# Low weight parts of the second layer kept in DRAM, and its second half's layer norm held until the gates are through

## The chip, the cores and the metric

The kernel runs on one core of one Trainium2 chip. The metric is device time in microseconds for one launch. TensorE (PE in the rows) multiplies; VectorE (DVE) and ScalarE (ACT) do the elementwise work; GpSimd (POOL) does a few small pieces; SyncE (SP) issues every DMA of this kernel, in one queue.

## The reference

Two layers over 2048 positions of 1024 features, all in float32. Layer 0 has attention and pooling branches; layer 1 is the convolution module that the change is about.

```
def odd_mixer(h, w_in, dw_w, dw_b, ln_g, ln_b, w_out):
    proj = h @ w_in
    a, b, gate = jnp.split(proj, [CONV_WIDTH, 2 * CONV_WIDTH], axis=-1)
    glu = a * jax.nn.sigmoid(b)
    conv = lax.conv_general_dilated(
        glu, dw_w.astype(glu.dtype), window_strides=(1,), padding=[(CONV_K - 1, 0)],
        dimension_numbers=('NWC', 'WIO', 'NWC'), feature_group_count=CONV_WIDTH)
    cf = conv.astype(jnp.float32) + dw_b.astype(jnp.float32)
    mu = jnp.mean(cf, axis=-1, keepdims=True)
    var = jnp.mean(jnp.square(cf - mu), axis=-1, keepdims=True)
    cn = (cf - mu) * lax.rsqrt(var + EPS) * ln_g.astype(jnp.float32) + ln_b.astype(jnp.float32)
    y = jax.nn.silu(cn).astype(h.dtype) * jax.nn.silu(gate)
    return y @ w_out
...
    for layer in range(DEPTH):
        h = rms_norm(x, pre_norm[layer])
...
        x = x + rms_norm(y, post_norm[layer])
```

## The kernel before

**Products in three matmuls.** Every float32 operand of a projection is held as a high part (rounded to `fp32r`) and a low part (the rest, also `fp32r`). A product is high times high, high times low and low times high: three matmuls of 128x512 for each of 8 slices of the contraction, 24 for one 128-feature output tile of 512 positions. For a weight of 128x1024 (512 KB), SP loads the raw tile `wr` (3 buffers), ACT copies it into the high part `wh` (2 buffers), and DVE subtracts to make the low part `wl` (2 buffers). `w_split` does that in the fixed order `wseq`; `project` takes the pair and issues the 24 matmuls.

**Stages.** The sequence is cut into two halves of 1024 positions, each into two blocks of 512 (b0, b1). Layer 0 does half 0 and half 1 in turn. In layer 1 each half goes through the input projections (`inproj1`, weights `wc` 0 to 15, each used for two blocks, so 48 matmuls a weight) and the gates (`gates1`, `wc` 16 to 23). Then comes the output projection (`outproj`, weights `wo1` 0 to 7): half 0 b0, half 0 b1, half 1 b0, each loading all 8 weights again, 24 matmuls a weight; and half 1 b1 as two pieces of 256 columns (`last_block`) that share one set of weights. So layer 1 loads and splits 48 + 32 = 80 weight tiles, though only 32 are different.

**The convolution and the norm.** Five of the eight feature tiles are convolved on DVE (`conv_dve`, 31 taps of 128x1024 each), three on TensorE (`conv_pe`). Results go to DRAM (`cd_*`, `ct_*`), the gates' values too (`sg_*`). `norms` loads the eight tiles of a half back (`s4` buffers), adds them for the mean, subtracts the mean and sums squares (`norm_block`), and then, tile by tile, `apply` multiplies by the reciprocal deviation, applies SiLU, multiplies by the gate and splits the product into high and low part (`mix`), which `outproj` multiplies. `post_norm` (tiles `xr`, `x1_*`, `out_y`) follows each output block.

**What sets the order.** A planner (`Flow`) writes the program while Python runs: generator tasks with priorities are stepped when the planner's own clocks say that their data are there; nothing is ordered by hand. A waiting task is stepped only when DVE and ACT are at most `LAG` ahead of TensorE in the plan. On the chip every engine then takes its list strictly in order. Buffers (`s4`: 37 of 4.2 KB a partition) are counted by `avail`, and a DMA into a buffer stands in SP's queue with a wait for the buffer's last reader. A weight's two buffers are free for weight n+2 when TensorE has done the last matmul of weight n.

Of the kernel before, what the change touches and what calls it, by code (L numbers as in the profile page):

```python
# [5 lines left out]
F32 = mybir.dt.float32  # L6
U8 = mybir.dt.uint8
F32R = mybir.dt.float32r
AF = mybir.ActivationFunctionType
ALU = mybir.AluOpType  # L10
# [31 lines left out]
    "mm": 4, "a0": 1, "a1": 1, "pt": 1, "pv": 1,  # L42
}
PACK = (
    ("sinks", 8), ("post", 2 * KT), ("icnt", 64), ("tri", 2 * P), ("pscale", 4), ("dwn", len(DVE_CONV) * CK), ("dwb", KT), ("dwbp", KT * GPT),
    ("lng", KT), ("lnb", KT),
)
LAG = 1.0
# [159 lines left out]
def trunk_kernel(tc, a):  # L208
# [38 lines left out]
    def get(tag, cols=TH, dt=F32):  # L247
        while avail[tag] <= 0:
            yield None
        if tag in ("a0", "a1", "pt", "pv") and freed[tag]:  # L250
            at = freed[tag][0]
            while avail[tag] <= 0 or at + MARGIN > flow.t["P"]:
                yield at if avail[tag] > 0 else None
                if freed[tag]:
                    at = freed[tag][0]
        return make(tag, cols, dt)
# [16 lines left out]
    def until(cond):  # L273
        while not cond():
            yield None
# [44 lines left out]
    for h in range(NH):  # L320
        wseq += [("wo1", f) for b in range(NB) for f in range(KT)]
    wraw, wready, last = [], [], set()

    def w_load(go):
        for n, (name, i) in enumerate(wseq):
# [29 lines left out]
    def w_split():  # L355
        for n in range(len(wseq), 0, -1):
            yield from until(lambda: wraw)
            name, i, raw, at = wraw.pop(0)
            yield from until(lambda: at)
            yield at[0]  # L360
            if name == "wut":
                raw = yield from fold(i, raw)
            if n > KT - 2 and n != len(wseq) - 2:
                wh = yield from get("wh", dt=F32R)
                wl = yield from get("wl", dt=F32R)
            else:
                yield from until(lambda: n > KT or len(last) == KT * NB)
                wh = (yield from get("s4", TH, F32R)).rearrange("p (k f) -> p k f", k=KT)
                wl = (yield from get("s4", TH, F32R)).rearrange("p (k f) -> p k f", k=KT)
            for j, ks in enumerate(WPARTS if n == len(wseq) else WHOLE):  # L370
                yield from until(lambda: len(at) > j)
                yield at[j]
                yield A.activation(wh[:, ks], raw[:, ks], AF.Copy)
                V.tensor_tensor(out=wl[:, ks], in0=raw[:, ks], in1=wh[:, ks].bitcast(F32), op=ALU.subtract)
                if j == 0:
                    wready.append((name, i, wh, wl))
            put(raw)
# [100 lines left out]
    def halves(t):  # L478
        return t[:, :BL], t[:, BL:]
# [100 lines left out]
    rb0 = {}  # L580
    flow.spawn(w_load(go), 0)
    flow.spawn(w_split(), 0)
    for b in range(NB):
        flow.spawn(prep_first(b, hs, have, go), 1 + b)
    flow.wait(lambda: len(go) == NB)
# [462 lines left out]
    def conv_pe(i, over):  # L1048
        gs, tts, nt = [], [], [0]
        for e in range(2):  # L1050
            g = (yield from get("s4", GPT // 2 * (GS + 2))).rearrange("x (r s) -> x r s", r=GPT // 2)
            G.memset(g[:, :, :2], 0.0)
            at = Q.dma_start(out=g[:, :, 2:], in_=gt[i][e * GPT // 2:(e + 1) * GPT // 2].rearrange("r x s -> x r s"))
            gs.append((g, at))
        for o in range(GPT // 4):
            bk = yield from get(f"a{o % 2}")
            for u in range(2):
                while len(tts) < 2 and nt[0] < GPT // 2:
                    tt = yield from get("s4", 2 * NJ * P)
                    r = 2 * nt[0]  # L1060
                    tts.append((tt, Q.dma_start(out=tt.rearrange("x (r n) -> x r n", r=2), in_=a["toep"][PE_CONV.index(i), r:r + 2].rearrange("r x n -> x r n"))))
                    nt[0] += 1
                tt, at = tts.pop(0)
                yield max(at, gs[o // 2][1])
                for v in range(2):
                    r4 = 2 * u + v
                    g = gs[o // 2][0][:, (o % 2) * 4 + r4]
                    for j in range(NJ):
                        at = T.matmul(bk[:, r4 * P:(r4 + 1) * P], tt[:, (v * NJ + j) * P:(v * NJ + j + 1) * P], g[:, 2 - j:2 - j + GS], start=j == 0, stop=j == NJ - 1)
                put(tt)  # L1070
            if o % 2:
                put(gs[o // 2][0])
            yield at
            co = yield from get("t2")
            for r4 in range(4):
                r = 4 * o + r4
                at = A.activation(co[:, r4 * P:(r4 + 1) * P], bk[:, r4 * P:(r4 + 1) * P], AF.Identity, bias=dwbp[:, i * GPT + r:i * GPT + r + 1], scale=1.0)
            put(bk)
            yield at
            Q.dma_start(out=cp_t[i][4 * o:4 * o + 4].rearrange("r x s -> x r s"), in_=co.rearrange("x (r s) -> x r s", r=4))  # L1080
            put(co)
        for h in range(NH):
            over[h].append(i)
# [51 lines left out]
    def apply(half, k, b, cfs, rbs, sgs, mix, done, left):  # L1135
        c = cfs[k][:, cols(b)]
        yield V.tensor_tensor(out=c, in0=c, in1=rbs[b], op=ALU.mult)
        yield A.activation(c, c, AF.Silu, bias=lnb[:, k:k + 1], scale=lng[:, k:k + 1])
        key = (k // 2, b)
        if key not in sgs:  # L1140
            yield from until(lambda: (half, *key) in stored)
            g = yield from get("s4")
            sgs[key] = (g, Q.dma_start(out=g, in_=sg_t[(half, *key)]))
        g, at = sgs[key]
        yield at
        yield V.tensor_tensor(out=c, in0=c, in1=halves(g)[k % 2], op=ALU.mult)
        t = yield from get("s4", TH, F32R)
        mix[b][k] = t
        hi, lo = halves(t)
        yield A.activation(hi, c, AF.Copy)  # L1150
        V.tensor_tensor(out=lo, in0=c, in1=hi.bitcast(F32), op=ALU.subtract)
        done.add((k, b))
        for tile, key in ((g, (k // 2, b)), (cfs[k], k)):
            left[key] = left.get(key, 0) + 1
            if left[key] == 2:
                put(tile)

    def norms(half, over, mix, done):
        yield from until(lambda: len(over[half]) >= 5 and (half == 0 or len(dones[half - 1]) >= KT))
        cfs, rbs, sgs, left, loaded = {}, {}, {}, {}, []  # L1160

        def load():
            for n in range(KT):
                yield from until(lambda: len(over[half]) > n)
                k = over[half][n]
                c = yield from get("s4")
                if k in DVE_CONV:
                    at = Q.dma_start(out=c, in_=cd_t[k, half])
                else:
                    view = cp_t[k].rearrange("r x s -> (r x s)").rearrange("(c q s) -> c q s", c=P, q=PH)  # L1170
                    at = Q.dma_start(out=c.rearrange("c (q s) -> c q s", q=PH), in_=view[:, :, half * SG:(half + 1) * SG])
                cfs[k] = c
                loaded.append((c, at))

        flow.spawn(load(), 1)
        total = yield from get("s4")
        for n in range(1, KT):
            yield from until(lambda: len(loaded) > n)
            c, at = loaded[n]
            yield at  # L1180
            V.tensor_tensor(out=total, in0=loaded[0][0] if n == 1 else total, in1=c, op=ALU.add)
        cfs["sum"] = total
        yield flow.t["V"]

        def block(b):
            yield from norm_block(b, cfs, rbs)
            yield from spread_tasks([apply(half, k, b, cfs, rbs, sgs, mix, done, left) for k in range(KT)], 3, 1 + b)
            put(rbs[b])

        for b in range(NB):  # L1190
            flow.spawn(block(b), 1 + b)
        yield from until(lambda: len(rbs) == NB)
        put(total)

    stored = set()

    def gate_out(half, j, b, sg, ready):
        yield from until(lambda: ready[0] == 2)
# [50 lines left out]
    for half in range(NH):  # L1249
        inproj1(half, hs, have, over)  # L1250
        now = hs
        hs, have = [{} for _ in range(NB)], [set() for _ in range(NB)]
        if half + 1 < NH:
            flow.spawn(prep(1, half + 1, hs, have, 2), 2)
        else:
            for h in range(NH):
                flow.spawn(norms(h, over, mixes[h], dones[h]), 1)
        gates1(half, now)
    for half in range(NH):
        outproj(1, half, mixes[half], dones[half])  # L1260
    flow.wait(lambda: not flow.tasks)
# [84 lines left out]
```

## Time and profile before

| what | us |
|---|---|
| median of 3 runs (1500.33 to 1501.77) | 1501.53 |
| the profiled execution, whole time | 1503.71 |
| its span, first to last instruction | 1500.8 |
| TensorE busy in the span (98%) | 1469.3 |
| VectorE busy (83%) | 1250.2 |
| ScalarE busy (38%) | 565.2 |

The profiled execution is one run; its whole time is its span and 2.9 us around it. "Busy" of TensorE counts an instruction from its start to its modelled end, so overlapping matmuls give a full share; pace is read better from the starts of successive matmuls. Idle time shows only as a gap between instructions.

### The profile page before, as it was taken

How to read it: one execution, taken by the hardware profiler on the slowest of the kernel's cores; microseconds unless marked ns; L12 is line 12 of the kernel's file. 1: busy time of each engine (PE TensorE's matmuls, PEld its weight loads, DVE VectorE, ACT ScalarE, POOL GpSimd, SP SyncE). 2: the span in 40 equal slices, each digit the busy share in tenths (PEclk: the TensorE clock that was granted, in tenths of full speed). 3: DMA queues.
4: the chain of work that ended last, by engine and by line, in shares of the span. 5: the costliest groups of instructions: out<-in, count | busy, mean ns of one | idle time of the engine just before them, and what ended most of it. 6: DMA issues, size and time to landing. Idle time of an engine off the chain costs nothing.

```text
span 1500.8 us, 19112 instructions
## 1 busy us (share of the span) xinstructions
PE 1469.3 (98%) x7226; PEld 1193.0 (79%) x7226; DVE 1250.2 (83%) x1927; ACT 565.2 (38%) x1069; POOL 49.1 (3%) x65
## 2 busy tenths in 40 slices
PE   8999999999999999999999999999999999998997
PEld 6877778788877778788888888888888888776796
DVE  7888775777887766577899999999999999989885
ACT  6454432454444423454211123211212134666551
POOL 0000000000000000000100000000000000000000
PEclk9999999999999999999999999999999999999898
DMA  6112312455411101355421224422544744836574
GB/s 221 57 54 80 97 44 59 140 175 176 145 33 33 46 29 56 99 178 187 166 63 55 82 85 136 172 71 67 182 148 137 236 144 137 256 127 229 165 251 154
DMA packets 107468, 186.46 MB, mean 124 GB/s; under 512 B 32240, under 2 KB 56432, under 8 KB 107376
## 3 DMA queue, kind: packets, MB, share of 16 engines
q1 hardware_dynamic: 107376, 185.25, 39.3%
q8 instruction: 56, 0.92, 0.3%
q14 instruction: 36, 0.29, 0.1%
HBM read 146.42 MB, written 38.80 MB: 123 GB/s over the span
## 4 chain that ended last, share of the span: by engine, by line
PE 92%; DVE 3%; DMA 2%; ACT 1%; issue 1%; SPq 0%; POOL 0%; POOLq 0%; DVEq 0%; ACTq 0%
PE mm L189 81%; PE a L189 5%; PE pv L189 3%; PE pt L189 2%; DVE s L189 2%; DMA s<-in_toep 1%; DVE t L189 1%; DVE wl L189 0%; DMA s<-in_xn 0%; DMA gt<-s 0%; ACT s L189 0%; DMA s<-sg 0%; SPq L189 0%; ACT wh L189 0%; ACT t L189 0%
## 5 line engine op out<-in xcount | busy, mean ns | idle before, releaser
L189 PE MATMUL mm<-s,wh 128*128 128x512 f32 (+1 forms) x3616 | 1139.6, 396 | 13.3 <-ACT s L189 7.4
L189 PEld LDWEIGHTS mm<-s,wh 128*128 128x128 f32 x3616 | 669.5, 189 | 164.6 <-DVE s L189 10.7
L189 PE MATMUL mm<-s,wl 128*128 128x512 f32 (+1 forms) x1808 | 709.9, 393 | 0.0
L189 PEld LDWEIGHTS mm<-s,wl 128*128 128x128 f32 x1808 | 341.4, 189 | 76.2
L189 DVE SCALAR_TENSOR_TENSOR s<-s,packed,s 128x1024 f32<-128x1024 f32 x290 | 354.6, 1279 | 0.0
L189 ACT ACTIVATE wh<-wr 128x1024 fp32r<-128x1024 f32 (+1 forms) x138 | 145.4, 1054 | 368.8 <-PE mm L189 315.9
L189 DVE TENSOR_TENSOR wl<-wr,wh 128x1024 fp32r<-128x1024 f32 (+1 forms) x138 | 167.7, 1215 | 74.9 <-ACT wh L189 72.8
L189 ACT ACTIVATE t<-mm 128x512 f32<-128x512 f32 (+1 forms) x122 | 68.5, 562 | 98.6 <-PE mm L189 90.3
L189 DVE TENSOR_TENSOR t<-t,t 128x512 f32<-128x512 f32 (+1 forms) x131 | 86.2, 663 | 17.3 <-ACT t L189 15.4
L189 ACT ACTIVATE s<-mm 128x512 f32<-128x512 f32 (+1 forms) x116 | 67.9, 585 | 78.2 <-PE mm L189 70.8
L189 PE MATMUL a<-s,s 128*128 128x128 f32 (+2 forms) x592 | 90.5, 290 | 1.1 <-DMA s<-in_toep 0.9
L189 PEld LDWEIGHTS a<-s,s 128*128 128x128 f32 x592 | 81.1, 190 | 11.1 <-DMA s<-in_toep 2.8
L189 DVE TENSOR_TENSOR s<-s,s 128x512 f32<-128x512 f32 (+3 forms) x100 | 85.0, 874 | 3.3 <-DMA s<-ct 1.0
L189 ACT ACTIVATE s<-t 128x512 fp32r<-128x512 f32 (+1 forms) x52 | 48.8, 938 | 64.4 <-DVE t L189 64.1
L189 DVE TENSOR_TENSOR s<-t,s 128x512 fp32r<-128x512 f32 (+1 forms) x56 | 52.4, 935 | 22.1 <-ACT s L189 20.9
L189 ACT ACTIVATE t<-s 128x512 f32<-128x512 f32 x80 | 48.8, 628 | 50.7 <-DVE s L189 42.4
L189 DVE TENSOR_TENSOR t<-pt,packed 128x512 f32<-128x512 f32 x64 | 44.1, 690 | 28.4 <-PE pt L189 27.9
L189 ACT ACTIVATE s<-s,st 128x128 f32<-128x128 f32 x128 | 49.6, 389 | 25.0 <-DVE st L189 24.9
L189 POOL TENSOR_TENSOR rs<-ms,mhalf 128x4 f32<-128x4 f32 (+1 forms) x21 | 24.9, 1186 | 791.8 <-DVE ms L189 787.7
L189 DVE SCALAR_TENSOR_TENSOR s<-t,mm 128x512 f32<-128x512 f32 x48 | 40.1, 836 | 8.1 <-PE mm L189 6.2
L189 ACT ACTIVATE s<-xh 128x512 fp32r<-128x512 f32 x48 | 29.9, 630 | 39.9 <-DVE xh L189 39.5
L189 PEld LDWEIGHTS pv<-t,s 128*64 128x64 f32 x480 | 25.1, 136 | 23.2 <-issue 7.2
(100 smaller groups left out, 928.3 us busy)
## 6 DMA issues: line engine op xcount, KB each, us to landing
wr<-in_wo SPq DMA_DIRECT2D x64, 512.0 KB, 3.7
wr<-in_wc SPq DMA_DIRECT2D x48, 512.0 KB, 3.7
wr<-in_wa SPq DMA_DIRECT2D x27, 512.0 KB, 3.7
s<-in_toep SPq DMA_DIRECT2D x24, 384.0 KB, 4.3
xr<-in_xp SPq DMA_DIRECT2D x32, 256.0 KB, 4.1
x<-s SPq DMA_DIRECT2D x32, 256.0 KB, 3.2
xh<-x SPq DMA_DIRECT2D x32, 256.0 KB, 3.6
sg<-s SPq DMA_DIRECT2D x16, 512.0 KB, 4.8
```

The source lines that it names most:

```text
L189: fn(*args, **kw)
```

## The change

Before, the low part of each layer-1 weight is made anew on DVE each time that the weight is used. Now a task `w_lows` of the lowest priority makes the 32 different ones once (load, ACT copy, DVE subtract) and stores them to DRAM; 29 are stored while layer 0 runs and three in the first projections of layer 1. In layer 1 `w_split` issues a 512 KB DMA into the `wl` buffer where DVE subtracted. Also, `norms` of half 1 starts when `gates1` of half 1 is written (`gated`) and no longer when half of half 0's products are there; each norm loads at most about three tiles ahead of its sum; half 1's norm tasks are one priority lower; `apply` leaves three `s4` buffers free before that point; and the bias table `dwbp` holds only the three convolutions on TensorE.

```diff
+    lows = [x for n, x in enumerate(wseq) if x[0] in ("wc", "wo1") and x not in wseq[:n]]
+    kept = {(name, i): dr.tile([P, KT, P], F32, tag=f"{name}l_{i}", name=f"{name}l_{i}") for name, i in lows}
+    formed = set()
+
+    def w_lows():
+        yield 60.0
+        for name, i in lows:
+            yield from until(lambda: avail["s4"] > 5)
+            raw = (yield from get("s4")).rearrange("p (k f) -> p k f", k=KT)
+            wl = (yield from get("s4", TH, F32R)).rearrange("p (k f) -> p k f", k=KT)
+            yield Q.dma_start(out=raw, in_=a[name][i])
+            yield A.activation(wl, raw, AF.Copy)
+            at = V.tensor_tensor(out=wl, in0=raw, in1=wl.bitcast(F32), op=ALU.subtract)
+            put(raw)
+            yield at
+            Q.dma_start(out=kept[name, i], in_=wl.bitcast(F32))
+            put(wl)
+            formed.add((name, i))
...
                 yield at[j]
+                if (name, i) in kept:
+                    yield from until(lambda: (name, i) in formed)
+                    Q.dma_start(out=wl.bitcast(F32), in_=kept[name, i])
                 yield A.activation(wh[:, ks], raw[:, ks], AF.Copy)
-                V.tensor_tensor(out=wl[:, ks], in0=raw[:, ks], in1=wh[:, ks].bitcast(F32), op=ALU.subtract)
+                if (name, i) not in kept:
+                    V.tensor_tensor(out=wl[:, ks], in0=raw[:, ks], in1=wh[:, ks].bitcast(F32), op=ALU.subtract)
...
+    flow.spawn(w_lows(), 6)
...
-            yield from until(lambda: (half, *key) in stored)
+            yield from until(lambda: (half, *key) in stored and (avail["s4"] > 3 or gated))
...
+        yield from until(lambda: avail["s4"] > 3 or gated)
         t = yield from get("s4", TH, F32R)
...
-        yield from until(lambda: len(over[half]) >= 5 and (half == 0 or len(dones[half - 1]) >= KT))
+        yield from until(lambda: len(over[half]) >= 5 and (half == 0 or gated))
...
-                yield from until(lambda: len(over[half]) > n)
+                yield from until(lambda: len(over[half]) > n and added[0] >= n - 2)
...
+            added[0] = n
...
-            flow.spawn(block(b), 1 + b)
+            flow.spawn(block(b), 1 + b + half)
...
         gates1(half, now)
+    gated.append(1)
```

Three places of the program show what moved. Names carry the buffer's number; `s4_` are the general buffers.

**DVE, at half 1 b0 of the output projection, before.** `wl_1732` is the low part of weight 1 for that block; `s4_1734` is the fourth of the block's eight products, `s4_1742`, `s4_1744` the next two; `ms_1743` belongs to the statistics of half 0 b1's output, which TensorE has finished when this block begins; between them stand pieces of `post_norm` (`xr_`).

```order
L189 TENSOR_TENSOR wl_1732_10910<-wr_1708_10770,wh_1731_10909 128x1024
L189 TENSOR_TENSOR s4_1734_10923<-s4_1589_10151,s4_1734_10923 128x512
L189 TENSOR_TENSOR s4_1624_10343<-s4_1624_10343,xr_1728_10887 128x512
...
L189 TENSOR_TENSOR t2_1662_10547<-t2_1662_10547,t2_1738_10947 128x512
L189 TENSOR_SCALAR ms_1743_10963<-pt_1740_10951 128x4
L189 TENSOR_TENSOR t2_1662_10547<-t2_1662_10547,t2_1741_10956 128x512
L189 TENSOR_TENSOR s4_1742_10961<-s4_1588_10149,s4_1742_10961 128x512
L189 TENSOR_TENSOR s4_1744_10970<-s4_1590_10153,s4_1744_10970 128x512
```

**DVE, the same place, now.** `s4_1813` and `s4_1814` are the seventh and eighth product of half 1 b0, `s4_1815` the first of b1; `ms_1825` is the same statistics of half 0 b1.

```order
L189 TENSOR_TENSOR s4_1813_11184<-s4_1681_10506,s4_1813_11184 128x512
L189 TENSOR_TENSOR s4_1684_10537<-s4_1684_10537,s4_1795_11094 128x512
L189 TENSOR_TENSOR s4_1651_10358<-s4_1651_10358,s4_1796_11101 128x512
L189 TENSOR_TENSOR s4_1653_10362<-s4_1653_10362,s4_1796_11101 128x512
L189 TENSOR_TENSOR s4_1814_11196<-s4_1684_10537,s4_1814_11196 128x512
L189 TENSOR_TENSOR s4_1815_11202<-s4_1651_10358,s4_1815_11202 128x512
...
L189 TENSOR_SCALAR ms_1825_11268<-pt_1824_11256 128x4
```

Five of the eight products stood behind the low part of weight 1; now all eight stand ahead of the statistics, and no low part is among them.

**SP, at the start of the output projection, now.** `wl_1646` is the low part of weight 1 and `wl_1659` that of weight 2 for half 0 b0; `cd_`, `ct_` are convolved tiles of half 1, `sg_0_` gates of half 0 that are loaded, `sg_1_3_1` one that is stored.

```order
L189 DMA wl_1646_10341<-wo1l_1_133 128x1024
L189 DMA wr_1649_10351<-in_wo1 128x1024
L189 DMA s4_1651_10358<-cd_0_1_79 128x1024
L189 DMA s4_1652_10360<-ct_2_75 128x16x64
L189 DMA s4_1653_10362<-cd_1_1_81 128x1024
L189 DMA s4_1655_10367<-sg_0_0_1_89 128x1024
L189 DMA s4_1656_10369<-sg_0_1_1_91 128x1024
L189 DMA sg_1_3_1_103<-s4_1632_10230 128x1024
L189 DMA wl_1659_10397<-wo1l_2_134 128x1024
```

Behind these stand `wr_1662`, `cd_3`, `ct_4`, then `wl_1667` (weight 3), `wr_1668`, an `sg_` load, `cd_5`, `wl_1677` (weight 4), `wr_1678`, `ct_6`, an `sg_` load, `cd_7` and `wl_1687` (weight 5). Before, the same loads of half 1 stand in one run there, with weights' raw tiles around them and no low part.

**SP, at the last block, now.** `s4_1886` and `s4_1887` are the residual input for its first piece, `wl_1890` the low part of weight 1.

```order
L189 DMA wl_1880_11570<-wo1l_0_132 128x1024
L189 DMA wr_1883_11580<-in_wo1 128x1024
L189 DMA s4_1886_11603<-x1_1_1_107 128x4x256
L189 DMA s4_1887_11604<-x1_1_1_107 128x4x256
L189 DMA wl_1890_11612<-wo1l_1_133 128x1024
L189 DMA wr_1892_11627<-in_wo1 128x1024
```

The residual loads stand ahead of a low part that did not go through this queue before.

## Rows read from the trace of the kernel before

**Rows 1.** The page's first lines: span, and busy us (share) of each engine.

```profile
span 1500.8 us, 19112 instructions
PE 1469.3 (98%) x7226; PEld 1193.0 (79%) x7226; DVE 1250.2 (83%) x1927; ACT 565.2 (38%) x1069; POOL 49.1 (3%) x65
```

**Rows 2.** Windows: stretch, length; busy (count) by engine; granted clock, DMA share, GB/s.

```profile
0.00:750.00 750.00, 739.25 (x3740) 588.26 (x3741) 560.52 (x1160) 329.24 (x684) 23.97 (x38) 1.00 0.33 104
750.00:1250.00 500.00, 498.97 (x2311) 410.75 (x2310) 478.39 (x449) 106.56 (x177) 15.63 (x20) 1.00 0.40 121
```

**Rows 3.** Windows of the output projection of layer 1, same columns.

```profile
1282.40:1328.90 46.50, 45.69 (x195) 36.31 (x194) 41.88 (x51) 26.77 (x41) 0.00 (x0) 1.00 0.78 239
...
1379.50:1403.90 24.40, 16.96 (x48) 12.06 (x48) 19.78 (x36) 9.94 (x15) 2.83 (x2) 0.65 0.49 169
1403.90:1439.90 36.00, 36.00 (x158) 29.29 (x157) 32.17 (x47) 22.49 (x35) 0.00 (x0) 1.00 0.72 231
```

**Rows 4.** Timeline of PE there: start, length, what, [idle before it, who ended it].

```profile
1380.86 0.50 PE L189 MATMUL mm<-s,wh 128*128 128x512 f32 x1 [0.89 <-DVE s L189]
...
1385.28 1.68 PE L189 MATMUL pt<-ones,t 128*128 128x1 f32 x8 [3.69 <-DVE t L189]
...
1389.41 0.80 PE L189 MATMUL mm<-s,wh 128*128 128x512 f32 x1 [1.14 <-DVE s L189]
```

**Rows 5.** Chain that ended last, one piece: start, length, matmuls run without a wait.

```profile
1287.72 30.48 PE mm L189 x132
```

**Rows 6.** Timeline of PE, undisturbed: eight one-column matmuls, then two spreading ones.

```profile
1349.91 0.95 PE L189 MATMUL pt<-ones,t 128*128 128x1 f32 x8
1350.72 0.70 PE L189 MATMUL pv<-s,onesr 128*128 128x512 f32 x2
```

**Rows 7.** Waits of PE, 750 us to the end: total, times, longest.

```profile
PE mm L189 <- DVE s L189: 4.6, 6, 1.1
```

**Rows 8.** The tile wl, 750 us to 1500: ns min/median/max, first and last start.

```profile
L189 DVE TENSOR_TENSOR wl<-wr,wh x69: 1202/1225/1233, 756.8 to 1441.0; 128x1024 fp32r<-128x1024 f32 x69
```

**Rows 9.** The tile wh, same stretch and columns: ACT's copy.

```profile
L189 ACT ACTIVATE wh<-wr x69: 1043/1062/1069, 755.6 to 1439.9; 128x1024 fp32r<-128x1024 f32 x69
```

**Rows 10.** Waits of PE in the first 750 us: total, times, longest.

```profile
PE pv L189 <- DVE t L189: 2.2, 3, 1.2
PE mm L189 <- DVE s L189: 1.3, 2, 0.6
```

**Rows 11.** DMA issues from 1332 to 1333 us, no other traffic: KB, us to landing.

```profile
wr<-in_wo SPq DMA_DIRECT2D x1, 512.0 KB, 3.5
```

**Rows 12.** Timeline of SP's issues in a burst (start, length of the issue).

```profile
1295.10 0.38 SPq L189 DMA_DIRECT2D s<-cd  x1
1295.57 0.53 SPq L189 DMA_DIRECT2D s<-ct  x1
1296.20 3.85 SPq L189 DMA_DIRECT2D s<-sg  x1
1300.14 0.38 SPq L189 DMA_DIRECT2D wr<-in_wo  x1
```

**Rows 13.** The same four issues, each in a window of its own: us to landing.

```profile
s<-cd SPq DMA_DIRECT2D x1, 512.0 KB, 5.3
s<-ct SPq DMA_DIRECT2D x1, 512.0 KB, 7.1
s<-sg SPq DMA_DIRECT2D x1, 512.0 KB, 7.7
wr<-in_wo SPq DMA_DIRECT2D x1, 512.0 KB, 5.0
```

**Rows 14.** Timeline of PE at the last block: its first two matmuls, and weight 1's.

```profile
1439.87 0.40 PE L189 MATMUL mm<-s,wh 128*128 128x256 f32 x2
...
1442.73 0.40 PE L189 MATMUL mm<-s,wh 128*128 128x256 f32 x2
```

**Rows 15.** DMA issues from 1437.5 to 1438.5 us: KB, median us to landing.

```profile
s<-x SPq DMA_DIRECT2D x2, 512.0 KB, 7.2
```

More of the change, by code (lines that the diff above doesn't have):

```diff
@@ L44 @@
 PACK = (
-    ("sinks", 8), ("post", 2 * KT), ("icnt", 64), ("tri", 2 * P), ("pscale", 4), ("dwn", len(DVE_CONV) * CK), ("dwb", KT), ("dwbp", KT * GPT),
+    ("sinks", 8), ("post", 2 * KT), ("icnt", 64), ("tri", 2 * P), ("pscale", 4), ("dwn", len(DVE_CONV) * CK), ("dwb", KT), ("dwbp", len(PE_CONV) * GPT),
     ("lng", KT), ("lnb", KT),
@@ L1076, in conv_pe @@
                 r = 4 * o + r4
-                at = A.activation(co[:, r4 * P:(r4 + 1) * P], bk[:, r4 * P:(r4 + 1) * P], AF.Identity, bias=dwbp[:, i * GPT + r:i * GPT + r + 1], scale=1.0)
+                at = A.activation(co[:, r4 * P:(r4 + 1) * P], bk[:, r4 * P:(r4 + 1) * P], AF.Identity, bias=dwbp[:, PE_CONV.index(i) * GPT + r:PE_CONV.index(i) * GPT + r + 1], scale=1.0)
             put(bk)
@@ L1158, in norms @@
     def norms(half, over, mix, done):
-        yield from until(lambda: len(over[half]) >= 5 and (half == 0 or len(dones[half - 1]) >= KT))
-        cfs, rbs, sgs, left, loaded = {}, {}, {}, {}, []
+        yield from until(lambda: len(over[half]) >= 5 and (half == 0 or gated))
+        cfs, rbs, sgs, left, loaded, added = {}, {}, {}, {}, [], [0]
         def load():
             for n in range(KT):
-                yield from until(lambda: len(over[half]) > n)
+                yield from until(lambda: len(over[half]) > n and added[0] >= n - 2)
                 k = over[half][n]
@@ L1186, in block @@
             yield from norm_block(b, cfs, rbs)
-            yield from spread_tasks([apply(half, k, b, cfs, rbs, sgs, mix, done, left) for k in range(KT)], 3, 1 + b)
+            yield from spread_tasks([apply(half, k, b, cfs, rbs, sgs, mix, done, left) for k in range(KT)], 3, 1 + b + half)
             put(rbs[b])
         for b in range(NB):
-            flow.spawn(block(b), 1 + b)
+            flow.spawn(block(b), 1 + b + half)
         yield from until(lambda: len(rbs) == NB)
         put(total)
-    stored = set()
+    stored, gated = set(), []
     def gate_out(half, j, b, sg, ready):
@@ L1324 @@
         "dwb": vec(dwb),
-        "dwbp": np.repeat(dwb.reshape(KT * GPT, GC).T, PH, axis=0),
+        "dwbp": np.repeat(dwb.reshape(KT, GPT * GC)[list(PE_CONV)].reshape(-1, GC).T, PH, axis=0),
         "toep": toep.reshape(len(PE_CONV), GPT, P, NJ * P),
```

## The prediction

> **What bounds the kernel now.** I read the page's first lines, then the windows by stage, then in the stage that stood out the timeline of TensorE, its waits, and SP's issues with their landings. TensorE is busy for 1469.3 of 1500.8 us [rows 1], so all that can be won is where it stands still or runs at its low clock. In the first 1250 us it stands idle for 12 us; in the convolution stage DVE is busy 478 of 500 us and TensorE still 499 [rows 2]: there a lighter DVE buys nothing by itself. The stage that stands out is the output projection of layer 1. In the 24.4 us from 1379.5 TensorE holds only 48 instructions, at a mean clock of 0.65 [rows 3]; (1 - 0.65) x 2 x 24.4 = 17 us of it ran at 1.2 GHz, the rest at 2.4. The reader should see there three idle gaps ended by DVE, the longest 3.69 us [rows 4]: TensorE waits for half 1 b0's products and for half 0 b1's sum of squares, and the low clock follows.
>
> The loss there: a long matmul starts every 30.48 / 132 = 0.231 us where nothing waits [rows 5], eight one-column ones take 0.81 us (1349.91 to 1350.72) [rows 6]. The 48 instructions are 27 long ones, 16 one-column ones and 5 of the spreading kind or cut by the window's edge, some 1.0 us: 6.2 + 1.6 + 1.0 = 8.9 us of work in 24.4, so 15.5 us lost. DVE ended 4.6 us of projection waits after 750 us [rows 7]; 3.2 of them lie in that stretch, 1.4 outside. **To be won: 17 us.**
>
> **What the change removes.** 80 subtractions of 1.22 us [rows 8] leave DVE in layer 1: 98 us; 29 of the 32 new ones run in layer 0. More to the point is where the products now stand. Before, five of the eight products of half 1 b0 stood behind weight 1's low part, among pieces of the post norm; in the new order all eight, and one of b1, precede the statistics of half 0 b1. TensorE can only produce these when it is done with the block before. So the products should be there when TensorE comes, and both gaps and the clock's fall go: -17. What is late next is no product but the new load.
>
> **What it adds: the low part comes over SP's queue.** It can't be issued before TensorE has left the buffer, at the end of weight n, and is needed at the third matmul of weight n+2: in the output projection 24 x 0.231 + 0.46 = 6.0 us later (in the input projections and gates 48 + 2 matmuls, 11.5 us, which covers the bursts too: I take nothing). A lone 512 KB lands 3.5 us after its issue [rows 11], so it is hidden when the queue is empty. In a burst it is not: issue time plus landing [rows 12, 13] gives landings at 1300.4, 1302.7, 1303.9 and 1305.1, one after the other in order of issue; a `ct_` tile takes 2.3 us, others 1.2. I use 1.3 per 512 KB (0.65 for 256 KB), 2.3 before the first byte counts, and walk through the order.
>
> First burst; 0 is the start of weight 0. `wl` of weight 1 is issued at 0 and lands at 3.6, `wr` (behind ACT's 1.06 us copy [rows 9]) at 4.9, then `cd_0` 6.2, `ct_2` 8.5, `cd_1` 9.8, two `sg_` 12.4, the stored `sg_` 13.7. Weight 2's `wl` may start at 5.5 and lands at 15.0; TensorE wants it at 11.55: **3.5 us of waiting**. The next: `wr` 16.3, `cd_3` 17.6, `ct_4` 19.9, weight 3's `wl` 21.2 against a need at 15.0 + 5.55 = 20.55: 0.6. Then `wr`, `sg_`, `cd_5`, weight 4's `wl` at 26.4, needed at 26.75: none. Then `wr`, `ct_6` 30.0, `sg_`, `cd_7` 32.6, weight 5's `wl` 33.9 against 32.3: 1.6. Together 5.8. Before, the same loads stood there and nothing of TensorE hung on them for its next weight; DVE made the low part.
>
> Half 1's loads beside the post norm of half 0 b0 (per weight `wl`, `wr`, mostly two `xr`, two `out_y`, half an `sg_`) come to about 5.2 us of queue in 5.55. The same walk gives one late `wl` (weight 7 of half 0 b1): 1.0.
>
> Last block: a weight now holds TensorE for 2.86 us (1439.87 to 1442.73 [rows 14]), and weight 1's `wl` stands behind both residual loads. These two landed 7.2 us (median) after issue [rows 15], behind other loads; with less ahead I take 6.0 for the second, issued 0.4 before the block: it lands at 5.6, `wl` at 6.9, needed at 2.86 + 0.24: 3.8 us.
>
> **Layer 0.** 29 formings add 29 x 1.22 = 35 us to DVE's 560 of 750 [rows 2] and as many copies of 1.06 to ACT, which is less than half busy. The task is the last to be stepped, but a subtraction in front of an urgent one delays it by up to 1.2 us. TensorE waited 3.5 us for DVE there [rows 10]; I add 1.0 (nothing to 4). Their 30 MB go at 104 GB/s mean, where one burst shows four times that [rows 12, 13]: hidden. The smaller bias table and the guards on buffers cost nothing: no work of TensorE hangs on them.
>
> Bounds of the waits: below, nothing, if all `wl` land like the lone one; above, each 512 KB counted at the slower pace of the mixed windows, 239 and 231 GB/s at DMA shares of 0.78 and 0.72 [rows 3], or 306 to 321 at a full share, 1.7 us: under rival C.
>
> **Sum:** -17 + 5.8 + 1.0 + 3.8 + 1.0 = -5.4. Against the profiled execution: span 1500.8 to 1495.4, its time 1503.7 to 1498.3. The median of the runs is 2.2 lower than that execution, so 1496.1.
>
> The Trainium skill ("DMA: Bandwidth & Descriptors", Specifications) gives about 358 GB/s of HBM for one core; the four landings here are faster, 512 KB in 1.2 us being some 430 GB/s. By the page a load would take 1.46 us, an estimate; the walk's waits would grow by about 2.5 us and the sum end at 1499. The measurement decides.
>
> **The rivals.**
> B, *the clock falls in the new waits.* The 3.69 us gap was followed by 17 us at the low clock [rows 3, 4]. Waits of 3.5 and 3.8 us are of that size; unlike before, TensorE then runs without gaps, so I price a fall at 4 us (at most the 25 long matmuls of that stretch at another 0.231 each, 5.8). Two falls: 1504. Against it: the earlier gap had a shorter one just ahead, 0.89 us. The Trainium skill ("TensorE: Matmul & The Clock Gate", Part 1) has the throttled state as the default that activity releases; by that rule this rival's time, 1504, holds, and the low clock right after the gap agrees.
> C, *the queue becomes the bound* (slower). Place: the 16 weights beside both post norms. At 1.7 us a load, the 5.2 us per weight become 6.8 for 5.55; each `wl` is then late by up to 1.2. Counting half of them late: 10 us more, 1506. It begins at 1.4 us a load and ends above 1504 from 1.5, half a microsecond at each of the 16. For it: the mean pace of the windows; against it: the four landings.
> D, *the loads are hidden anyway*: without the walk's 10.6 us, 1485.5. For it: stretches of the burst where more than one load shares the engines would land earlier than my one-by-one queue says; against it: rows 12 and 13 are one by one.
> E, *the change doesn't do what it says:* half 1's norm, held for the gates, is late as before. Then the 15.5 stay, and with the waits it is 1511.6. Against it: the order of DVE.
>
> **Numbers.** Likeliest, A, is the sum: 0.42. B 0.20, C 0.15, D 0.15, E 0.08. A measurement of this kernel tells 0.2%, 3 us, from no change. A by itself spans 1491 to 1501: three quarters faster, a quarter same. B: a tenth faster, 0.45 same, 0.45 slower. C: a fifth same, the rest slower. D faster. E slower. That makes 0.49 faster, 0.23 same, 0.28 slower. The range reaches to D's and C's times: 1486 to 1507.
>
> **What the profile after would show.** Right: no gap of TensorE ended by DVE at half 1 b0; gaps of some 3.5 us ended by a DMA into `wl` at weight 2 and at weight 1 of the last block; DVE's busy time down by 48 x 1.22 = 59 us, DMA bytes up by 144 x 0.524 = 75 MB. Wrong: low clock in those gaps (B); small waits at nearly every weight of the output projection (C); none (D); gaps ended by DVE still there (E), or a layer 0 that is longer by more than 4 us.

## The result, and the profile after

The changed kernel takes 1510.24 us (median of 4 runs, 1508.97 to 1513.97) against 1501.65 (1500.33 to 1502.59) of the kernel before on the same chip: ratio 1.0062, 95% interval 1.0042 to 1.0082. It is slower by 0.6%, where 0.4% faster was forecast. The profiled execution took 1511.22 us, its span 1509.4; before they were 1503.71 and 1500.8 [rows 1].

The page's first lines, and its line of DMA bytes:

```profile
span 1509.4 us, 19347 instructions
...
PE 1470.7 (97%) x7226; PEld 1194.1 (79%) x7226; DVE 1194.2 (79%) x1879; ACT 594.8 (39%) x1101; POOL 48.4 (3%) x65
...
DMA packets 128493, 262.99 MB, mean 174 GB/s; under 512 B 34576, under 2 KB 58768, under 8 KB 128400
```

DVE is lighter by 56.0 us (59 forecast), and the bytes went from 186.46 MB on the page of before to 262.99, 76.5 MB more (75 forecast). So the work moved as it was meant to. The two largest waits of TensorE, from 750 us to the end (total, times, longest):

```profile
PE mm L189 <- DMA wl<-wo1l: 17.5, 6, 6.3
PE pv L189 <- DVE s L189: 1.9, 1, 1.9
```

The 4.6 us of waits for DVE before projections [rows 7] are gone; in their place there are 17.5 us of waits for the new load. The timeline of TensorE has the six (idle before and its releaser at the end of the row):

```profile
1297.93 0.80 PE L189 MATMUL mm<-s,wl 128*128 128x512 f32 x1 [6.28 <-DMA wl<-wo1l]
1317.47 0.50 PE L189 MATMUL mm<-s,wl 128*128 128x512 f32 x1 [1.19 <-DMA wl<-wo1l]
1365.01 0.50 PE L189 MATMUL mm<-s,wl 128*128 128x512 f32 x1 [1.98 <-DMA wl<-wo1l]
1385.37 0.50 PE L189 MATMUL mm<-s,wl 128*128 128x512 f32 x1 [1.81 <-DMA wl<-wo1l]
1424.35 0.80 PE L189 MATMUL mm<-s,wl 128*128 128x512 f32 x1 [2.49 <-DMA wl<-wo1l]
1448.98 0.58 PE L189 MATMUL mm<-s,wl 128*128 128x256 f32 x1 [3.80 <-DMA wl<-wo1l]
```

In order they are weights 2 and 5 of half 0 b0, 4 and 7 of half 0 b1, 5 of half 1 b0, and 1 of the last block. Windows of the clock behind them, and one of the old stall's place (stretch, length; busy by engine; granted clock, DMA share, GB/s):

```profile
1291.60:1297.90 6.30, 0.06 (x1) 0.00 (x0) 5.24 (x8) 3.58 (x7) 0.00 (x0) 0.70 1.00 345
1297.90:1301.00 3.10, 3.07 (x7) 2.48 (x8) 2.51 (x5) 2.18 (x3) 0.00 (x0) 0.51 1.13 336
1301.00:1317.00 16.00, 15.29 (x66) 12.02 (x64) 10.09 (x13) 7.24 (x11) 0.00 (x0) 1.00 1.07 353
1365.90:1369.20 3.30, 3.30 (x9) 2.54 (x8) 3.30 (x7) 1.90 (x4) 0.00 (x0) 0.50 0.83 245
1386.40:1389.60 3.20, 3.20 (x9) 2.43 (x8) 3.20 (x6) 1.50 (x3) 0.00 (x0) 0.50 1.02 406
1423.90:1427.20 3.30, 2.85 (x7) 2.27 (x8) 0.11 (x1) 0.00 (x0) 0.00 (x0) 0.50 0.98 354
1449.00:1454.50 5.50, 5.50 (x26) 5.50 (x27) 1.70 (x5) 1.06 (x1) 1.01 (x1) 0.50 1.02 405
1394.20:1401.70 7.50, 7.50 (x38) 6.29 (x37) 5.83 (x12) 5.68 (x9) 1.01 (x1) 1.00 0.75 269
```

Five of the six waits are followed by a stretch at 1.2 GHz in which TensorE works at half pace: 3.1, 3.3, 3.2, 2.85 and 5.5 us of busy time, of which half is lost, 9.0 us. With the gaps that makes 26.5 us.

The last of these rows is where [rows 3] had 48 instructions in 24.4 us. The tenth projection matmul of half 1 b0 and the one 27 further on stand at 1379.48 and 1403.93 before, at 1394.24 and 1401.80 now: 24.45 us became 7.56, **16.9 us** less. Of these, 1.3 us are work that moved and no loss: 16 one-column and 4 spreading matmuls stood in that stretch, and 8 and 2 of them now stand in the block before. So 15.6 us of loss went there, for 15.5 forecast. The two waits before it (0.81 and 0.57 us) went too; together that is the forecast 17.

The balance: the output projection starts 2.5 us earlier than before (1279.89 for 1282.37). An idle time is counted from a modelled end; from start to start of the matmuls around them, less the usual step (0.231 us, half of it in the last block), the six gaps cost 18.5 us and not 17.5. So -2.5 - 17.0 + 18.5 + 9.0 = +8.0, and the span is longer by 8.6. The other 0.6 us were not placed.

### The profile page after: what moved, and what is told of

It reads as the page before. It is cut to its first block, busy times and chain, and to the rows that moved or that the text cites. A ratio compares the mean times of both kernels' runs of the same rounds, so it can differ in the third digit from the quotient of the medians.

```text
span 1509.4 us, 19347 instructions
## 1 busy us (share of the span) xinstructions
PE 1470.7 (97%) x7226; PEld 1194.1 (79%) x7226; DVE 1194.2 (79%) x1879; ACT 594.8 (39%) x1101; POOL 48.4 (3%) x65
## 2 busy tenths in 40 slices
DMA packets 128493, 262.99 MB, mean 174 GB/s; under 512 B 34576, under 2 KB 58768, under 8 KB 128400
## 5 line engine op out<-in xcount | busy, mean ns | idle before, releaser
L189 PE MATMUL mm<-s,wl 128*128 128x512 f32 (+1 forms) x1808 | 713.2, 394 | 17.5 <-DMA wl<-wo1l 17.5
L189 DVE TENSOR_TENSOR s<-s,s 128x512 f32<-128x512 f32 (+4 forms) x132 | 123.9, 958 | 30.7 <-DMA s<-sg 10.6
L189 DVE TENSOR_TENSOR t<-t,t 128x512 f32<-128x512 f32 (+1 forms) x131 | 86.0, 663 | 49.7 <-ACT t L189 47.9
L189 DVE TENSOR_TENSOR wl<-wr,wh 128x1024 fp32r<-128x1024 f32 (+1 forms) x64 | 77.2, 1206 | 37.2 <-ACT wh L189 36.1
L189 ACT ACTIVATE s<-s 128x1024 fp32r<-128x1024 f32 (+1 forms) x64 | 53.1, 843 | 41.2 <-DMA s<-in_wc 16.7
L189 ACT ACTIVATE s<-s,st 128x128 f32<-128x128 f32 x128 | 49.4, 388 | 12.2 <-DVE st L189 12.1
L189 DVE TENSOR_TENSOR s<-s,xr 128x512 f32<-128x512 f32 x56 | 37.4, 688 | 14.5 <-DMA xr<-x 7.4
```

The costliest lines, as they stand in the source:

```text
L189: fn(*args, **kw)
```

## Experiments

Three theories were put against each other. **Theory 1:** waits for `wl` are local prices, paid since its buffer comes free late; take one away and its price is won. **Theory 2:** the DMA engines (or SP's queue) carry more than they can while the norms' tiles are loaded, so that a load added there costs by itself. **Theory 3:** the planner had room to write half 1's products ahead of TensorE because its own clock counted the waits for `wl`; without them it writes the products late, and the old stall returns. Medians are of the runs named, beside runs of the kernel before on the same chip (1500.3 to 1501.0 us); ratios with their 95% interval.

### Parts of the change, and more time for the load

```diff
-    "wr": 3, "wh": 2, "wl": 2,
+    "wr": 2, "wh": 2, "wl": 3,
```

> Three buffers for wl instead of two, and two for wr instead of three (the memory of one for the other); all else as in the change. Theory 1 (each late low part is late only because its buffer comes free at the end of weight n; gap and low clock behind it cost 29 us in all): a load can now be issued one weight, 24 matmuls of 0.231 = 5.5 us, earlier, so the 6.28 us wait becomes under 1 us and the ones of 1.2 to 3.8 us vanish: 1480 to 1486 us. Theory 2 (SP's queue and the DMA engines carry more than they can beside the norms, whatever the buffers): the waits stay within a third, 1500 to 1510.

**1500.82 us, ratio 1.0007 (0.9997 to 1.0017).** Gaps for `wl` fell to 10.4 us, the wait of 6.28 only to 4.6. The time is 9.4 us below the change's and in Theory 2's range, though the waits went down by more than a third. The edit did less than it said: the load is written behind the wait for a `wh` buffer, which is freed as before. A run below sets that right.

```diff
+        for k in order if late else ():
+            T.matmul(out, wl[:, k, :], src(k, b)[0][:, part], start=False, stop=k == order[-1])
```

> In the output projection of layer 1 the eight matmuls with wl come after the sixteen with wh, so wl is needed 14 matmuls (3.2 us; 1.5 us in the last block) later; loads and buffers as in the change. Theory 1: waits of 1.2 to 2.5 us vanish with the low clock behind them, 6.28 becomes 3.1, 3.80 becomes 2.3; some of half 1 b0's products come late again, since TensorE wants all eight within 16 matmuls: 1490 to 1497. Theory 2: loads that are late because the queue is full stay late from weight to weight, 1503 to 1510.

**1506.26 us, 1.0044 (1.0029 to 1.0059).** One wait for `wl` was left, 3.6 us, near to what Theory 1 has; the time is in Theory 2's range all the same, for 10.1 us of waits for DVE and ACT came up before projections, all of them at half 1 b0. What was won on one side was lost on the other: the first sign of Theory 3.

```diff
-    lows = [x for n, x in enumerate(wseq) if x[0] in ("wc", "wo1") and x not in wseq[:n]]
+    lows = []
```

> No low part is kept: DVE subtracts as before, and only the new timing of the norms is left of the change. Theory 1 (the relief of DVE in the output projection cured the stall at half 1 b0): all eight products stand behind low parts again and the stall of 15 us is back: 1499 to 1506. Rival (the timing of the norms alone cured it): 1484 to 1489.

**1508.33 us, 1.0058 (1.0043 to 1.0073).** The new timing of the norms does not cure the stall, and costs on its own: waits in the output projection of

```profile
PE mm L189 <- ACT s L189: 8.7, 3, 4.5
PE mm L189 <- DVE s L189: 4.6, 7, 2.4
```

```diff
-    lows = [x for n, x in enumerate(wseq) if x[0] in ("wc", "wo1") and x not in wseq[:n]]
+    lows = [x for n, x in enumerate(wseq) if x[0] == "wc" and x not in wseq[:n]]
```

> Low parts are kept for the input projections and gates only; in the output projection DVE subtracts as before. Theory 1: no wait for wl in the output projection (-29 us against the change), but the stall at half 1 b0 is back (+15): 1494 to 1500. Rival (the timing of the norms alone cured the stall): 1480 to 1486. Theory 2 (the wc loads cost by themselves in the convolution stage): some us more than either.

**1507.15 us, 1.0050 (1.0035 to 1.0065).** No gap for `wl`, but 12.1 us of waits for ACT and DVE, nearly all at half 1 b0. So it isn't enough to lighten DVE ahead of the output projection. The times forecast for this run and the one before were too low.

### Is it the wait, the bytes or the order?

The load is issued ahead of the `wh` buffer's wait, with three `wl`:

```diff
             if n > KT - 2 and n != len(wseq) - 2:
-                wh = yield from get("wh", dt=F32R)
                 wl = yield from get("wl", dt=F32R)
...
+            if (name, i) in kept:
+                yield from until(lambda: (name, i) in formed)
+                Q.dma_start(out=wl.bitcast(F32), in_=kept[name, i])
+            yield at[0]
```

> Three wl and two wr buffers as in the run before, and the load of a low part is now written as soon as a wl buffer is free, ahead of the wait for a wh buffer, which had held it back to the old place. Theory 1 (waits for wl and the stall at half 1 b0 are independent costs): waits for wl under 4 us in all, 1481 to 1488 us. Theory 3 (the waits gave the planner room to put half 1's products ahead of TensorE; without them products are late again, and what was won there is paid back): 5 to 12 us of waits for DVE and ACT return at half 1 b0, 1489 to 1498. Theory 2 (queue or bandwidth full): over 1500.

**1512.38 us (1507.96 to 1514.0), 1.0079 (1.0063 to 1.0096).** Waits for `wl` are down to 3.1 us, so the load has its time now; but 11 us of waits for DVE and ACT are back at half 1 b0, and the whole is no faster. The time is in Theory 2's range, the waits are Theory 3's. Theory 1 is refuted as a rule for all waits: taking one away can bring back another.

Next the wait alone is taken away, and then the loads too. These two runs and the next two leave the weights' low part out of the output projection's result; they are read for their time alone.

```diff
-            T.matmul(out, wl[:, k, :], hi, start=False, stop=k == order[-1])
+            T.matmul(out, (wh if same else wl)[:, k, :], hi, start=False, stop=k == order[-1])
```

> In the output projection of layer 1 the third matmul reads wh where it read wl; every wl load is still issued, and nothing of TensorE waits for it. So the low part of the weight is left out of that projection's result. Theory 1: 17.5 us of gaps and some 9 us of their low clock go: 1481 to 1486. Theory 3: products of half 1 late again, 1489 to 1498. Theory 2: the traffic itself costs, over 1500.

> As the run before, and the 32 loads of low parts for that projection are not issued either. If the traffic costs something by itself (Theory 2), this is over 3 us faster than the run before; if only the wait for a load costs (Theories 1 and 3), it is within 3 us of it.

**1504.54 us, 1.0026 (1.0016 to 1.0035)** with loads that nobody reads, **1490.60, 0.9931 (0.9916 to 0.9946)** without them. With them TensorE meets the old stall again, nine gaps from 1378.05 to 1398.64, of which three:

```profile
1383.22 1.40 PE L189 MATMUL pv<-s,onesr 128*128 128x512 f32 x2 [3.03 <-DVE s L189]
1386.29 0.80 PE L189 MATMUL mm<-s,wh 128*128 128x512 f32 x1 [1.67 <-ACT s L189]
1388.16 1.65 PE L189 MATMUL mm<-s,wh 128*128 128x512 f32 x3 [1.07 <-DVE s L189]
```

14 us lie between the two, but two things differ: the bytes, and, since the planner counts every load, the order that it wrote. The next two runs hold one fixed and change the other.

```diff
+                        nc.sync.dma_start(out=wl[:, :1].bitcast(F32), in_=kept[name, i][:, :1])
+                        flow.note("S", 4.0 * P * KT * P / 360e3, [kept[name, i]], [wl])
```

> The program of the run in which the low parts are loaded for the output projection and not read (1504.5 us), in the same order on every engine; each of these 32 loads now moves one of its eight slices, 64 KB for 512. So the low part is left out of that projection here too. If the bytes cost (Theory 2: half 1's norm loads wait behind them in the queue), its 14 us go for the most part: 1488 to 1494, as without loads. If the planner's order costs (Theory 3: it wrote half 1's products later), it stays at 1501 to 1506.

**1504.33 us, 1.0024 (1.0012 to 1.0035).** An eighth of the bytes in the same order gains nothing. The window of the stall's place (same columns as above) in the run with whole loads, and then in this one:

```profile
1376.00:1402.00 26.00, 14.40 (x36) 7.86 (x35) 23.73 (x41) 13.51 (x23) 1.32 (x1) 0.56 0.71 248
```

```profile
1376.00:1402.00 26.00, 14.06 (x40) 7.92 (x39) 23.93 (x42) 13.49 (x22) 1.32 (x1) 0.65 0.66 230
```

In this order it is the order that costs: DVE is busy 24 of 26 us there, with pieces of the post norm among half 1's products. In the run without loads (1490.6 us) the same stretch is:

```profile
1376.00:1402.00 26.00, 23.81 (x98) 18.61 (x97) 19.57 (x34) 16.66 (x27) 1.32 (x1) 0.93 0.55 187
```

Why the planner wrote the slow order isn't shown. Theory 3's reason, that products come late once no wait for `wl` is counted, doesn't fit the run without loads: its planner counted no such wait either, and only 2.2 us of waits stand at half 1 b0 there. Now the fast order, with the whole loads put in unplanned and unread:

```diff
-                        Q.dma_start(out=wl.bitcast(F32), in_=kept[name, i])
+                        nc.sync.dma_start(out=wl.bitcast(F32), in_=kept[name, i])
```

> The reverse: the program of the run without these loads (1490.6 us), in the same order, with the 32 loads of 512 KB put into it, unread, and not counted by the planner. If the bytes cost: 1499 to 1506. If the order costs: 1489 to 1494.

**1500.06 us, 0.9993 (0.9984 to 1.0003):** 9.5 us more than in that order without them. Here the loads cost, though TensorE waits for none of them. It waits for the norm, as the largest of its rows for 1280 to 1460 us show:

```profile
PE a L189 <- DVE s L189: 2.4, 1, 2.4
PE mm L189 <- DVE s L189: 2.4, 2, 2.0
PE mm L189 <- ACT wh L189: 1.0, 1, 1.0
```

That the norm's tiles landed later for the loads' bytes, and not for their places in SP's queue, is argued and not shown: slices were not run in this order. So the loads cost as Theory 2 has it, and the order costs as Theory 3 has it (its reason apart), each in an order of its own. The costs don't add: 13.7 us for the order with slices, 9.5 for the loads in the fast order, 13.9 for both.

Is it SP's one queue, or the DMA engines behind it? The loads go to a queue of ACT's, with the order of TensorE, DVE and POOL unchanged:

```diff
-                    Q.dma_start(out=wl.bitcast(F32), in_=kept[name, i])
+                    (Q if name == "wc" else A).dma_start(out=wl.bitcast(F32), in_=kept[name, i])
```

> The change, with the 32 loads of the output projection's low parts issued by ACT into a DMA queue of its own; the order on TensorE, DVE and ACT is the same. If the low parts are late because they stand behind the norm's tiles in one queue, in order: gaps for wl fall from 17.5 us to under 6, and with their low clock 15 us are won; what the norm's loads lose comes back as a wait at half 1 b0 of up to 8: 1492 to 1503. If the DMA engines are full whatever the queue: gaps stay over 12 us, 1505 to 1512.

**1510.07 us, 1.0066 (1.0051 to 1.0081).** Gaps for `wl` fell from 17.5 to 10.2 us, between the two forecasts; the time is that of full engines, since the norm's tiles paid for it:

```profile
PE mm L189 <- DMA wl<-wo1l: 10.2, 6, 3.9
PE pt L189 <- DVE t L189: 3.4, 1, 3.4
PE a L189 <- DVE s L189: 2.3, 1, 2.3
```

Its window from 1285 us has the engines full, with two queues; below it is the same window of the change:

```profile
1285.00:1315.00 30.00, 24.92 (x100) 19.49 (x99) 18.94 (x26) 15.05 (x23) 0.00 (x0) 0.94 1.08 357
```

```profile
1285.00:1315.00 30.00, 23.72 (x97) 18.84 (x96) 17.91 (x24) 14.75 (x22) 0.00 (x0) 0.89 1.04 331
```

A second queue found the engines full already: 357 GB/s for 331, and no time won. The Trainium skill ("DMA: Bandwidth & Descriptors", Queues, rings and completion order) says that SP's and ACT's queues are rings on the same 16 engines; the shares of 1.04 and 1.08 and the unchanged time (1510.07 for 1510.24) agree.

### The timing of the norms, and fewer loads

`norms` and `apply` have the conditions and priorities of before, all low parts are kept:

```diff
-        yield from until(lambda: len(over[half]) >= 5 and (half == 0 or gated))
+        yield from until(lambda: len(over[half]) >= 5 and (half == 0 or len(dones[half - 1]) >= KT))
```

> All low parts kept, and the norms with the conditions and priorities of the kernel before. If DVE's relief alone cured the stall at half 1 b0, the stall stays away and the wl waits remain: 1505 to 1513 us. If the new timing of the norms was needed with it, the stall is back beside the waits: 1515 to 1527.

**1503.66 us, 1.0020 (1.0010 to 1.0031).** The stall stays away, so the new timing was not needed: in this order the relief of DVE is enough, as it was not in the three above in which the stall came back. The time is a little under the forecast. One wait stands out, weight 2 of the first block:

```profile
1304.27 0.80 PE L189 MATMUL mm<-s,wl 128*128 128x512 f32 x1 [10.05 <-DMA wl<-wo1l]
```

> All low parts kept, the norms as in the kernel before (1503.7 us, with one wait of 10 us for wl at weight 2), and the 32 loads issued by ACT into a queue of its own. One queue as the cause: the 10 us wait shrinks below 4 and the time falls to 1488 to 1497. Full DMA engines as the cause: 1500 to 1506.

**1504.03 us, 1.0033 (1.0020 to 1.0046).** The wait shrank to 0.7 us, and the matmul for the norm's mean just behind it waited 6.65 us for DVE instead. From 1283 to 1303 us the DMA share is 1.02 with one queue and with two: the engines are full, whatever the queue.

Then the loads were cut where they meet the burst (weights counted down by `n`; the last block is `n <= 8`):

```diff
+                use = (name, i) in kept and (name == "wc" or 8 < n <= 24)
+                if use:
...
-                if (name, i) not in kept:
+                if not use:
                     V.tensor_tensor(out=wl[:, ks], in0=raw[:, ks], in1=wh[:, ks].bitcast(F32), op=ALU.subtract)
```

> Of the output projection's four blocks only the two in the middle (half 0 b1, half 1 b0) load low parts; the first and the last subtract on DVE as before. If the waits are local prices, the 10 us lost in the first block and the 6.8 at the last go and the middle stays: 1491 to 1496. If the planner's order trades them (three of half 1 b0's products now stand close before TensorE), half of it is paid back there: 1497 to 1504.

**1488.74 us (1487.70 to 1489.89), 0.9923 (0.9907 to 0.9940):** 0.8% faster than the kernel before, with a full result, and below both forecasts. Its waits from 1280 to 1460 us, all of them:

```profile
PE mm L189 <- DMA wl<-wo1l: 2.0, 2, 1.4
PE mm L189 <- DVE s L189: 0.2, 1, 0.2
```

and two stretches, the burst and half 1 b0 (which starts at 1376.3 here), with the change's burst below them:

```profile
1280.00:1310.00 30.00, 30.00 (x131) 24.34 (x130) 22.74 (x28) 17.61 (x27) 0.00 (x0) 1.00 0.88 272
1372.00:1402.00 30.00, 29.52 (x129) 23.02 (x128) 26.43 (x45) 21.22 (x34) 1.44 (x1) 1.00 0.90 331
```

```profile
1280.00:1310.00 30.00, 23.72 (x97) 18.85 (x96) 17.61 (x24) 14.75 (x22) 0.00 (x0) 0.89 0.98 316
```

In the burst DVE has the time to subtract (22.74 of 30 us) and the engines carry less (0.88 for 0.98). In the middle DVE is spared. The engines are no emptier there (0.90), yet all waits for low parts come to 2.0 us; no convolved tiles are loaded in that stretch, but no run shows that this is the reason.

> The same choice of blocks, with the norms' timing of the kernel before (all low parts loaded: 1503.7 us, one wait of 10 us in the first block, 2.4 at the last). No product of half 1 b0 stands close before TensorE in its program. Local prices: 1486 to 1492, faster than the kernel before and than any run with a full result so far. Trade: the subtractions in the first block make half 1's norm late, 1496 to 1504.

**1491.28 us, 0.9940 (0.9922 to 0.9958):** the same choice of blocks wins with the old timing of the norms too.

```diff
+                use = (name, i) in kept and (name == "wc" or n > 8)
```

> The change, with the last block alone subtracting on DVE. All before it stays, and its wait of 3.8 us with the low clock behind it goes: 6 to 7 us less than the change, 1503 to 1505. If the subtractions come late there for the two pieces of 256 columns, it gains nothing, 1508 to 1511.

**1506.51 us, 1.0040 (1.0025 to 1.0055).** The wait at the last block is gone, and the gaps for `wl` fell by its 3.8 us, to 13.7. From its first projection matmul to its last, that block takes 47.9 us for 54.5: 6.6 us with its clock, a local price here, as forecast. Of the whole, 5.8 us are left by the profiled spans (1503.6) and 3.7 by the medians, under the 6 to 7 expected: the blocks before it have the program of the change, but other waits in this execution.

```diff
+                use = (name, i) in kept and (name == "wc" or n % 2)
```

> The norms' timing of before, and low parts loaded for every second weight of the output projection (1, 3, 5, 7), subtracted for the others: half the bytes, spread out. If full DMA engines in the first block are what makes a low part late, the 10 us wait falls by half or more: 1493 to 1498. If any load behind the norm's tiles is as late, whatever their number: 1500 to 1504.

**1503.16 us, 1.0019 (1.0009 to 1.0028).** Half the bytes, and the wait at weight 3 of the burst is still 8.2 us. Number matters less than place: with half as many, a load behind the norm's tiles is still late.

## Why the prediction was wrong, point by point

The step that failed is the price of TensorE's waits for `wl`: 10.6 us in the sum, with nothing for the clock behind them; the runs showed 17.5 us of gaps and 9.0 us of low clock. The gain came as forecast.

**To be won, 17 us: right**, 15.6 at the place named and 1.4 at two waits before it, and the reason held in the change (no product behind a low part; the two runs in which DVE subtracts there, without low parts and with those of `wc` alone, have the stall). What was not seen is how much hangs on the planner's order: three others with all these loads in them (low parts read last; loaded early; loaded and not read) brought the stall back without a single subtraction there.

**First burst, 5.8 us: too small, 7.5 of gaps.** Landings after, one issue each (weight 1's `wl`, `wr` behind it, weight 2's `wl`; us to landing), issued at 1280.08, 1280.93 and 1289.70:

```profile
wl<-wo1l SPq DMA_DIRECT2D x1, 512.0 KB, 3.3
...
wr<-in_wo SPq DMA_DIRECT2D x1, 512.0 KB, 6.0
```

From the start of weight 0 at 1279.89 they landed at 3.5, 7.0 and 18.0 us (8.2 after the issue); the walk had 3.6, 4.9 and 15.0. So 2.1 of the 3.0 us were lost at the second load, for which the walk took the 1.3 us of a train, and 0.9 on the tiles between. Weight 2 then waited 6.28 for 3.5, weight 3 nothing for 0.6, weight 5 1.19 for 1.6.

**Beside the post norm, 1.0 us: too small, 6.3.** Weight 7 of half 0 b1 was named and waited 1.81; weight 4 there (1.98) and weight 5 of half 1 b0 (2.49) were counted as hidden. In order of time the three that waited (1.98, 1.81, 2.49) landed 8.4, 7.1 and 6.9 us after their issue, where TensorE leaves 6.0 at most: the walk had too little ahead of them. Ahead of the first stood two `sg_` loads where the walk had half a one, and a raw tile that landed 4.3 us behind a lone low part.

**Last block, 3.8 us: right**, 3.80, but in part by luck: from the block's start the second residual tile landed at 4.4 us for the walk's 5.6, and the low part 2.6 us behind it for 1.3.

**The clock: the largest step that failed.** It stood in rival B, two falls at 4 us, 0.20, and not in the sum. Five waits were followed by a fall, also those of 1.81 and 1.98 us, at 1.4 to 2.8 us each: 9.0 us. Rival B had the mechanism; its total (8 us) is near by luck, with two falls for five and 4 us for 1.4 to 2.8. The Trainium skill's rule cited there ("TensorE: Matmul & The Clock Gate", Part 1: the throttled state is the default) agrees with the rows: behind five of the waits the granted clock is 0.50 or 0.51.

So the terms for `wl` are 17.5 us of gaps for 10.6, and 9.0 for their clock instead of none: 15.9 us, more than the whole difference of 14 between 1495.4 and 1509.4. **Layer 0, +1.0:** wrong in sign. Forming added no wait of TensorE for DVE: these waits in the first 750 us, 3.5 us in [rows 10], are

```profile
PE mm L189 <- DVE s L189: 1.1, 2, 0.6
PE pv L189 <- DVE t L189: 0.5, 1, 0.5
PE a L189 <- DVE st L189: 0.3, 1, 0.3
```

The matmul that starts at 697 us before starts 4.4 us earlier in the change, and 3.2 us earlier in the run without low parts, which forms nothing. So most of that gain isn't due to forming; the one thing that was changed for layer 0 in that run is the smaller bias table, and what it did to the order was not looked into. Of the gain, 2.5 us were left at the output projection.

**Rival C** (the queue becomes the bound) was right in its core, as the runs with unplanned loads and with ACT's queue show, but not in its place: three of its 16 weights waited, and the largest wait is in the burst. The 358 GB/s of the Trainium skill ("DMA: Bandwidth & Descriptors", Specifications) fits the stretches of the burst, 336 to 353 GB/s with the `ct_` tiles among them; of the full windows without these, two have 405 and 406, above that figure, and one 354. Four landings in a row were too short a sample. **D** and **E** did not come.

## What to carry to other kernels

Work that is taken from a busy engine and given to the DMA queue is won only where the loads land in time: choose by stage, as in the fastest run here, not for all uses of a tile. Price a short wait of TensorE with the slow stretch behind it. And where a planner's clock writes the order, a wait taken away changes the order too: hold the order fixed with one run before reading a cause from another.

## What the chip showed that was not expected

A raw tile issued 0.9 us behind a lone low part lands much later than alone. Landings from 750 us on, before (up to 1282 us) and after (up to 1280):

```profile
wr<-in_wc SPq DMA_DIRECT2D x40, 512.0 KB, 3.8
```

```profile
wl<-wcl SPq DMA_DIRECT2D x43, 512.0 KB, 3.4
...
wr<-in_wc SPq DMA_DIRECT2D x40, 512.0 KB, 5.1
```

By these medians that is 5.1 + 0.9 - 3.4 = 2.6 us from landing to landing (pair by pair, the median of 42 is 2.4), where a train has 1.2 to 1.3. What makes it so stays open.

The clock: behind the gap of 1.19 us here, and one of 1.41 us in the fastest run, the granted clock stayed at 1.00; behind 1.81 us it fell to 0.50, and stayed there after TensorE was busy again. Length alone does not decide it: behind a gap of 2.33 us in the run with ACT's queue (at 1321.00), and one of 2.67 us in the run with the early loads (at 1466.96), it stayed at 1.00, behind one of 1.80 us in the run with the two middle blocks and the old timing (at 1380.21) it fell. In the prediction's sum a wait counted as its own length; in the change those of 1.8 to 2.5 us each cost 1.4 to 1.7 us more in the slow stretch behind them.
